# Modulation columns by two transposes per step, with shift and scale formed on VectorE

## The chip, the core and the metric

The kernel runs on one core of a Trainium2 chip. The metric is the device time of one execution in microseconds (us). Three runs of the kernel before took 601.96, 602.42 and 602.82 us, so the median is 602.42 us. The engines are named as the profile names them: PE is TensorE's matmul, PEld its weight load, DVE is VectorE, ACT is ScalarE, POOL is GpSimd, SP is SyncE, whose queue issues most of the transfers here.

## What is computed

One layer of a diffusion trunk: an adaLN-modulated RMSNorm, an input projection, two head groups (a gated position mixer and a latent attention), and an output projection. Only the modulation matters here. For each of the two conditioning vectors, `c` for 1024 latent tokens and `c_ctx` for 128 context tokens:

```python
mod = jax.nn.silu(cond) @ w_ada + b_ada
shift, scale, gate = jnp.split(mod[:, None, :], 3, axis=-1)
h = _rmsnorm(x, norm_g) * (1 + scale) + shift
u, v, g_a, c_q, c_kv, k_rope, g_b = _split_in(h @ w_in)
```

The width is 1024, handled as eight blocks of 128 channels (k = 0 to 7). Each token tile is transposed, so that channels lie on partitions; shift and scale of a block are therefore wanted as columns, one number per partition.

## The kernel before

The change lies in the start of the program, roughly its first 50 us. There are nine token tiles of 128 (g = 0 is tiles 0 to 2, g = 1 tiles 3 to 5, g = 2 tiles 6 to 8). For each block k the start does the following.

- **rows** (`mod_rows`, L337): eight products of the conditioning vector's columns (`csp`, padded with zeros to 32 columns) with the modulation weights (`ada`) go to four strips of 32 partitions in `modp`, columns 0 to 255, each strip holding the sum over two of the eight input blocks. In a strip, row 0 belongs to one conditioning vector, row 1 to the other, and the rest is zero.
- **copy** (`mod_copy`, L341): DVE copies these 256 columns to SBUF (`rows`).
- **cols** (`mod_cols`, L345): two f32 matmuls with `rows` as weights and `sel` (a 128x2 matrix of ones that picks row 0 or 1 of each strip) as the moving operand add the four strips and turn them to columns at once. They write `modp[:, 256:260]`.
- **act** (`mod_act`, L348 and L349): two ACT operations read these columns from PSUM and make shift and scale in `at`, the first by adding a bias, the second by a scale and a bias.
- **hh, hf, lo**: ACT applies `at` to the transposed tile (L571, rounded to fp32r, the high part), ACT or DVE does it again in f32 (L578 on ACT, L580 on DVE), and DVE subtracts to get the low part (L112).
- **va, vb**: PE multiplies the high parts (L431, L432) and the low parts (L436) of the tiles with the weights of v, which accumulate over k in the banks `vacc`. Those weights are split by POOL into a high part (**wh**, L115) and a low part (**wl**, L550).

The transposes of the token tiles (L353) are `xT` and `xe`; they use tiles that were first scaled by the RMSNorm root (**sc**: L389 on ACT, L393 on DVE, L391 on POOL). For tiles 3 to 5 these go to ACT, DVE and POOL in turn (the constant `SC1 = "SVG"`).

All of this shares one PSUM bank, `modp`. From block 2 on, one step of the planner, `group(k)`, issues cols of k, the transposes of group 1, and rows of k+1, in this order, and act of k is issued behind them.

The order on each engine is not written by hand. `start_steps` lists steps with an engine, a cost, dependencies and a priority; `Plan.run` plays them forward against these costs and issues each step when its turn comes. A changed cost or engine in the list thus changes the order of other steps too, and each engine then keeps its order whatever the chip does. The SP queue issues loads in a fixed order, and a load into a buffer that is still read waits at the head of that queue: the weights of v for block k+2 (`wvr`, L309) wait for wl of block k, and the modulation weights behind them wait as well.

Of the kernel before, what the change touches and what calls it, by code (L numbers as in the profile page):

```python
# [9 lines left out]
F32 = mybir.dt.float32  # L10
# [3 lines left out]
AF = mybir.ActivationFunctionType  # L14
ALU = mybir.AluOpType
AX = mybir.AxisListType
PSUM = bass.MemoryType.PSUM

P = 128
NT = 9  # L20
NS = 8
NK = 8
# [72 lines left out]
def tile_hymba_step(ctx: ExitStack, tc: tile.TileContext, I, O):  # L95
    nc = tc.nc
    V, S, G, T = nc.vector, nc.scalar, nc.gpsimd, nc.tensor

    def opened(name, bufs=1, space=None, side=None):
        kw = dict(name=name, bufs=bufs, reuse_waits="tile")  # L100
        if space is not None:
            kw["space"] = space
        if side is not None:
            kw["side"] = side
        cm = tc.tile_pool(**kw)
        return cm, cm.__enter__()
# [4 lines left out]
    def lo_of(lo, src, hi):  # L111
        V.tensor_tensor(lo, src, f32(hi), op=ALU.subtract)  # L112
# [58 lines left out]
    def catch_up(until):  # L171
        at_ = now[0]
        while waiting and waiting[0][0] <= until:
            due, fn = waiting.pop(0)
            now[0] = due
            fn()
        now[0] = at_
# [9 lines left out]
    def step(cost, fn):  # L187

        catch_up(now[0])
        for f in list(fill):  # L190
            if f[0] in made and made_at[f[0]] <= now[0]:
                fill.remove(f)
                run(f[1:])
        run((cost, fn))
# [12 lines left out]
    def run(step):  # L207
        catch_up(now[0])
        step[1]()
        now[0] += step[0]  # L210
# [23 lines left out]
    ident = pc.tile([P, P], F32, tag="ident", name="ident")  # L234
# [8 lines left out]
    normg = cst[:, 16:24]  # L243
    badaT = cst[:, 24:48].rearrange("p (k j) -> p k j", j=3)
# [3 lines left out]
    at = pc.tile([P, 8, 2, 2], F32, tag="at", name="at")  # L248
    gbias = pc.tile([P, 8], F32, tag="gbias", name="gbias")
# [13 lines left out]
    c_vb, vb = opened("vb", side="left")  # L263
# [12 lines left out]
    sel = va.tile([P, 2], F32, tag="sel", name="sel")  # L276
# [51 lines left out]
    mps, rowsb = {}, {}  # L328

    modp = psa.tile([P, 512], F32, tag="acc", name="modp")  # L330

    def mod_rows(k, i):


        for j in range(4):
            kk = 4 * i + j
            T.matmul(modp[32 * j : 32 * j + 32, 0:256], csp[:, kk, :], ada[k][kk], start=i == 0, stop=i == 1)  # L337

    def mod_copy(k):
        rowsb[k] = va.tile([P, GW], F32, tag="tm", name=f"rows{k}", bufs=2)[:, :256]  # L340
        V.tensor_copy(rowsb[k], modp[:, 0:256])  # L341

    def mod_cols(k):
        for c in range(2):
            T.matmul(modp[:, 256 + 2 * c : 258 + 2 * c], rowsb[k][:, c * P : (c + 1) * P], sel, start=True, stop=True)  # L345

    def mod_act(k):
        S.activation(at[:, k, :, 0], modp[:, 256:258], AF.Identity, bias=badaT[:, k, 0:1])  # L348
        S.activation(at[:, k, :, 1], modp[:, 258:260], AF.Identity, bias=gbias[:, k : k + 1], scale=normg[:, k : k + 1])  # L349

    def transposes(k, ts_, ps):
        for j, t in enumerate(ts_):
# [54 lines left out]
    def h_pe(k, g):  # L407
        xps[k, g] = pst.tile([P, 512], F32, tag="t", name=f"xT{k}{g}")
        transposes(k, [3 * g, 3 * g + 1, 3 * g + 2], xps[k, g])
# [24 lines left out]
    def last_product(k, t):  # L434
        g, j = t // 3, t % 3
        T.matmul(vacc[t], hl[k, g][:, j * P : (j + 1) * P], wvh[k], start=False, stop=False)  # L436
# [3 lines left out]
    def keep_warm(n):  # L440
        for _ in range(n):
            T.matmul(warm[:, 0:P], ident, ones, start=True, stop=True)

    def start_steps(plan):
        step = plan.add
# [95 lines left out]
        def split_hi(k):  # L541
            wvh[k] = wide(1024 * k, 512)
            if k == 0:
                S.copy(wvh[k], wvr[k])
            else:
                pool_copy(wvh[k], wvr[k])

        def split_lo(k):
            wvl[k] = wide(1024 * k + 512, 512)
            G.tensor_tensor(wvl[k], wvr[k], f32(wvh[k]), op=ALU.subtract)  # L550
# [3 lines left out]
        def both_rows(k):  # L554
            mod_rows(k, 0)
            mod_rows(k, 1)

        def group(k):
            mod_cols(k)
            h_pe(k, 1)  # L560
            if k + 1 < NK:
                both_rows(k + 1)

        def plan_alias(key, *others):
            for o in others:
                plan.alias.setdefault(key, []).append(o)

        def high(k, g):
            src = first_t(k) if g == 0 and k > 0 else xps[k, g][:, :GW]
            b_, a_ = at[:, k, 0, 0:1], at[:, k, 0, 1:2]  # L570
            S.activation(hh[k, g], src, AF.Identity, bias=b_, scale=a_)  # L571
# [10 lines left out]
        for k in range(NK):  # L582
            q = 0.1 * k
            step(f"wh{k}", "S" if k == 0 else "G", 0.62, lambda k=k: split_hi(k), [f"wv{k}"], 1 + q)
            step(f"wl{k}", "G", 1.28, lambda k=k: split_lo(k), [f"wh{k}"], 1 + q)
            if k == 0:
                step("fill", "T", 0.0, lambda: keep_warm(2), ["rows0.1"], 0)
                for i in range(2):
                    step(f"rows0.{i}", "T", 0.45, lambda i=i: mod_rows(0, i), [f"ada0.{i}", *(["rows0.0"] if i else [])], 1)
                step("cols0", "T", 0.5, lambda: mod_cols(0), ["copy0"], 0)  # L590
            elif k == 1:
                step("rows1.1", "T", 0.7, lambda: both_rows(1), ["ada1.0", "ada1.1", "copy0", "cols0"], 1.1)
            step(f"copy{k}", "V", 0.42, lambda k=k: mod_copy(k), [f"rows{k}.1"], 0.2 + q)
            if k == 1:
                step("cols1", "T", 0.5, lambda: mod_cols(1), ["copy1", "act0"], 1.0)
                for q_ in range(2):
                    step(f"xt{q_}1", "T", 0.36, lambda q_=q_: h_pe(q_, 1), [*scaled[1], "cols1"], 1.1 + 0.1 * q_, takes=("pst",))
                step("rows2.0", "T", 0.45, lambda: mod_rows(2, 0), ["copy1", "ada2.0", "xt11"], 1.2)
                step("rows2.1", "T", 0.45, lambda: mod_rows(2, 1), ["rows2.0", "ada2.1", "va03"], 1.2)
            elif k > 1:  # L600

                step(
                    f"cols{k}", "T", 0.8 + (0.65 if k + 1 < NK else 0.0), lambda k=k: group(k),
                    [f"copy{k}", f"act{k - 1}", *scaled[1], *([f"ada{k + 1}.{i}" for i in range(2)] if k + 1 < NK else [])], 1 + q, takes=("pst",),
                )
                plan_alias(f"cols{k}", f"xt{k}1", *([f"rows{k + 1}.1"] if k + 1 < NK else []))
            step(f"act{k}", "S", 0.6, lambda k=k: mod_act(k), [f"cols{k}"], 0.2 + q)
            for g in range(2):
                pre = g == 0 and k > 0
                if k == 0 and g == 0:  # L610
                    step(f"xt{k}{g}", "T", 0.36, lambda k=k, g=g: h_pe(k, g), [*scaled[g], *([f"act{k - 1}"] if k > 1 else [])], 2 + q, takes=("pst",))
                src = f"xs{k}" if pre else f"xt{k}{g}"
                e_ = FULL[g] if k else "SV"[g]
                step(f"hh{k}{g}", "S", 0.6, lambda k=k, g=g: high(k, g), [src, f"act{k}"], 2 + q)
                last = () if pre else ("pst",)
                step(f"hf{k}{g}", e_, {"S": 0.6, "V": 0.66, "G": 0.6}[e_], lambda k=k, g=g, e_=e_: full(k, g, e_), [src, f"act{k}", f"hh{k}{g}", *([f"lo{k}0"] if g and k > 3 else [])], 2.05 + q, gives=last)
                step(f"lo{k}{g}", "V", 0.58, lambda k=k, g=g: lo_of(hl[k, g], hf[k, g], hh[k, g]), [f"hf{k}{g}"], 2.1 + q)
                if k == NK - 1:
                    continue
                for t in (0, 1, 2) if g == 0 else (3, 4):  # L620
                    before = [f"va{k - 1}{t}"] if k else []
                    if (k, t) == (1, 0):
                        before.append("va03")
                    step(f"va{k}{t}", "T", 0.46, lambda k=k, t=t: first_products(k, t), [f"hh{k}{g}", f"wl{k}", *before], 3 + q + 0.001 * t, takes=("psa",) if k == 0 else ())
                    step(f"vb{k}{t}", "T", 0.23, lambda k=k, t=t: last_product(k, t), [f"lo{k}{g}", f"va{k}{t}"], 3 + q + 0.01 + 0.001 * t)

    engines = {mybir.EngineType.PE, mybir.EngineType.Activation, mybir.EngineType.DVE, mybir.EngineType.Pool}
    with tc.manual_schedule(engines=engines):
        keep_warm(WARM0)
        start = Plan()  # L630
# [9 lines left out]
    step = plan.add  # L640
# [589 lines left out]
    for g in range(3):  # L1230
        q = area[g].rearrange("p (s h) c -> p s h c", s=4)
# [830 lines left out]
    step = plan.add  # L2062
# [111 lines left out]
    for q in range(3, len(queue)):  # L2174
        n, name, _ = queue[q]
# [278 lines left out]
```

## Time and profile before

| | us |
|---|---|
| median of three runs | 602.42 (601.96 to 602.82) |
| the profiled execution's own time | 602.15 |
| its span, first to last instruction | 600.4 |
| PE busy | 590.3 |
| DVE busy | 427.3 |
| ACT busy | 329.2 |
| POOL busy | 214.0 |

The profiled execution lies 1.75 us above its own span and 0.27 us below the median. A row of a timeline reads: start, duration, engine, line, operation, output<-inputs, the number merged, and in brackets how long the engine had been idle and what released it. Consecutive matmuls overlap, so the distance between starts, not the duration, is what one costs.

### The profile page before, as it was taken

The page shows a single profiled execution, that of the slowest core. Times are in us where ns is not written, and L with a number is a line of the kernel's source. Part 1 is how long each engine was busy: PE and PEld are TensorE (multiplying, and loading weights), DVE is VectorE, ACT ScalarE, POOL GpSimd, SP SyncE. Part 2 cuts the span into 40 slices and gives each one's busy share as a digit, 9 for nine tenths or more (in the row PEclk, how much of TensorE's full clock was granted, in tenths as well). Part 3 has the DMA queues.
Part 4 walks back from the last instruction along what each step waited for, and adds up shares of the span by engine and source line. Part 5 has one row for each costly group of instructions (what it writes and reads, how often), then busy time and mean ns, then how long its engine had stood idle before and what let it go on. Part 6 is the DMA issues. An engine that isn't in the chain of part 4 may idle for free.

```text
span 600.4 us, 10191 instructions
## 1 busy us (share of the span) xinstructions
PE 590.3 (98%) x3661; PEld 528.2 (88%) x3661; DVE 427.3 (71%) x940; ACT 329.2 (55%) x773; POOL 214.0 (36%) x251
## 2 busy tenths in 40 slices
PE   9999999999999999999999999999999999999995
PEld 8578889999989999999998888888888898888884
DVE  4666888977647368476678677778788876477885
ACT  6565886434323245465577566656656462457543
POOL 2571103200000000343363345454544547269834
PEclk9999999999999999999999999999999999999998
DMA  8991001032052134100002033434242029951444
GB/s 319 370 370 70 1 2 70 1 140 71 4 212 69 69 93 138 43 1 0 2 8 71 0 106 106 157 126 141 81 143 94 1 72 303 361 178 41 144 147 160
DMA packets 31059, 67.33 MB, mean 112 GB/s; under 512 B 3344, under 2 KB 17440, under 8 KB 29984
## 3 DMA queue, kind: packets, MB, share of 16 engines
q1 hardware_dynamic: 27792, 55.93, 26.9%
q0 software_dynamic: 2352, 8.39, 4.1%
q10 hardware_dynamic: 864, 2.36, 1.1%
q8 instruction: 29, 0.48, 0.3%
q14 instruction: 22, 0.18, 0.1%
HBM read 53.45 MB, written 13.21 MB: 111 GB/s over the span
## 4 chain that ended last, share of the span: by engine, by line
PE 93%; DMA 3%; DVE 2%; ACT 1%; POOL 1%; issue 0%; SPq 0%; POOLq 0%; ACTq 0%
PE p L916 14%; PE tp L937 7%; PE pT L1586 6%; PE o L1610 3%; PE o L1612 3%; PE o L1611 3%; PE zacc L1349 2%; PE zacc L1348 2%; PE zacc L1350 2%; PE S L1947 2%; PE S L1948 2%; PE S L1949 2%; DMA ada<-in_ada_ss 2%; PE s L1503 2%; PE s L1506 2%; PE s L1505 2%
## 5 line engine op out<-in xcount | busy, mean ns | idle before, releaser
L1463 POOL TENSOR_SCALAR e<-e,rs 128x1280 f32<-128x1280 f32 x32 | 47.0, 1468 | 97.2 <-DVE rs L1462 62.8
L112 DVE TENSOR_TENSOR pl<-pT,ph 128x512 fp32r<-128x512 f32 x81 | 55.5, 687 | 32.5 <-ACT ph L1590 32.2
L1458 ACT ACTIVATE e<-s,nb,scl 128x256 f32<-128x256 f32 x64 | 56.9, 890 | 38.9 <-DVE nb L1446 26.2
L1590 ACT CAST ph<-pT 128x512 fp32r<-128x512 f32 x80 | 47.1, 589 | 40.8 <-PE pT L1586 40.6
L1196 POOL TENSOR_TENSOR kr<-z,rope 128x64 f32<-128x64 f32 x8 | 2.6, 324 | 155.3 <-ACT z L1205 155.3
L937 PE MATMUL tp<-area,w 128*128 128x384 f32 x288 | 52.6, 338 | 0.0
L1610 PE MATMUL o<-ph,vh 128*128 128x256 f32 x160 | 50.7, 317 | 0.0
L937 PEld LDWEIGHTS tp<-area,w 128*128 128x128 f32 x288 | 50.4, 188 | 0.0
L1586 PE MATMUL pT<-ident,e 128*128 128x128 f32 x320 | 48.0, 273 | 0.0
L1586 PEld LDWEIGHTS pT<-ident,e 128*128 128x128 f32 x320 | 38.9, 140 | 7.2
L1612 PE MATMUL o<-ph,vl 128*128 128x256 f32 x160 | 45.1, 282 | 0.0
L1611 PE MATMUL o<-pl,vh 128*128 128x256 f32 x160 | 44.9, 280 | 0.0
L1440 DVE TENSOR_REDUCE m<-s 128x1 f32<-128x1024 f32 x32 | 39.0, 1218 | 2.6 <-PE s L1481 2.5
L1610 PEld LDWEIGHTS o<-ph,vh 128*128 128x128 f32 x160 | 30.2, 189 | 4.7 <-ACT os L1620 2.9
L1611 PEld LDWEIGHTS o<-pl,vh 128*128 128x128 f32 x160 | 30.4, 190 | 0.4
L1612 PEld LDWEIGHTS o<-ph,vl 128*128 128x128 f32 x160 | 30.1, 188 | 0.0
L916 PE MATMUL p<-area,w 128*128 128x384 f32 x144 | 27.7, 339 | 0.0
L916 PE MATMUL p<-area,s 128*128 128x384 f32 x144 | 27.3, 337 | 0.0
L1348 PE MATMUL zacc<-w1t,area 128*128 128x448 f32 x72 | 27.1, 376 | 0.0
L916 PE MATMUL p<-w1t,s 128*128 128x384 f32 x144 | 26.9, 339 | 0.0
L1349 PE MATMUL zacc<-w1t,area 128*128 128x448 f32 x72 | 26.3, 366 | 0.0
L1350 PE MATMUL zacc<-w1t,area 128*128 128x448 f32 x72 | 26.3, 365 | 0.0
(697 smaller groups left out, 1770.4 us busy)
## 6 DMA issues: line engine op xcount, KB each, us to landing
ada<-in_ada_ss SPq DMA_DIRECT2D x16, 512.0 KB, 6.0
w2r<-in_w_t SPq DMA_DIRECT2D x12, 512.0 KB, 5.1
x<-in_x SPq DMA_DIRECT2D x9, 512.0 KB, 8.4
adag<-in_ada_g SPq DMA_DIRECT2D x4, 1024.0 KB, 4.8
traw<-in_w_o SPq DMA_DIRECT2D x16, 256.0 KB, 3.8
tdram<-thi SPq DMA_DIRECT2D x32, 128.0 KB, 1.9
tdram<-traw SPq DMA_DIRECT2D x32, 128.0 KB, 1.8
wor<-in_w_o SPq DMA_DIRECT2D x8, 512.0 KB, 3.8
```

Source lines behind the costliest of these rows:

```text
L112: V.tensor_tensor(lo, src, f32(hi), op=ALU.subtract)
L916: T.matmul(banks[key], a_, b_, start=k == 0 and m == 0, stop=k == 3 and m == len(passes) - 1)
L937: T.matmul(tps[c, 2][:, :GW], w_[c][:, k, :], x_[k, 2], start=k == 0 and m == 0, stop=k == NK - 1 and m == 2)
L1348: T.matmul(ps[:, :448], a, wqh[k], start=k == 0, stop=False)
L1440: V.tensor_reduce(m[:, 0:1], lat_, axis=AX.X, op=ALU.max)
L1458: S.activation(e[:, sl], src, AF.Exp, bias=nb, scale=scl[:, t : t + 1], accum_out=su[:, i : i + 1])
L1463: G.tensor_scalar(e, e, rs, 0.0, op0=ALU.mult, op1=ALU.add)
L1586: T.transpose(ps[:, w : w + P], es[t, h][:, c * P : (c + 1) * P], ident)
L1590: later(0.5, lambda: S.copy(ph[:, :w], ps[:, :w]))
L1610: T.matmul(o, vh[:, kt, :], ph[:, sl], start=c == 0, stop=False)
L1611: T.matmul(o, vh[:, kt, :], pl[:, sl], start=False, stop=False)
L1612: T.matmul(o, vl[:, kt, :], ph[:, sl], start=False, stop=c == n - 1)
```

## The change

The diff, whole:

```diff
     def mod_cols(k):
         for c in range(2):
-            T.matmul(modp[:, 256 + 2 * c : 258 + 2 * c], rowsb[k][:, c * P : (c + 1) * P], sel, start=True, stop=True)
+            T.transpose(modp[:, 256 + c * P : 256 + (c + 1) * P], rowsb[k][:, c * P : (c + 1) * P], ident)
 
     def mod_act(k):
-        S.activation(at[:, k, :, 0], modp[:, 256:258], AF.Identity, bias=badaT[:, k, 0:1])
-        S.activation(at[:, k, :, 1], modp[:, 258:260], AF.Identity, bias=gbias[:, k : k + 1], scale=normg[:, k : k + 1])
+        m = vb.tile([P, 2, 2], F32, tag="mods", name=f"mods{k}", bufs=2)
+        V.tensor_reduce(m, modp[:, 256:512].rearrange("p (a j c) -> p a c j", a=2, j=4)[:, :, 0:2, :], axis=AX.X, op=ALU.add)
+        V.tensor_scalar(at[:, k, :, 0], m[:, 0, :], badaT[:, k, 0:1], None, op0=ALU.add)
+        V.tensor_scalar(at[:, k, :, 1], m[:, 1, :], normg[:, k : k + 1], gbias[:, k : k + 1], op0=ALU.mult, op1=ALU.add)
...
-                step("cols0", "T", 0.5, lambda: mod_cols(0), ["copy0"], 0)
+                step("cols0", "T", 0.35, lambda: mod_cols(0), ["copy0"], 0)
...
-                step("cols1", "T", 0.5, lambda: mod_cols(1), ["copy1", "act0"], 1.0)
+                step("cols1", "T", 0.35, lambda: mod_cols(1), ["copy1", "act0"], 1.0)
...
-                    f"cols{k}", "T", 0.8 + (0.65 if k + 1 < NK else 0.0), lambda k=k: group(k),
+                    f"cols{k}", "T", 0.65 + (0.65 if k + 1 < NK else 0.0), lambda k=k: group(k),
...
-            step(f"act{k}", "S", 0.6, lambda k=k: mod_act(k), [f"cols{k}"], 0.2 + q)
+            step(f"act{k}", "V", 0.55, lambda k=k: mod_act(k), [f"cols{k}"], 0.2 + q)
```

The two matmuls with `sel` become two transposes of the same rows, which fill columns 256 to 511 of `modp` with four strips side by side. DVE adds the strips (a reduction of 16 numbers to 4 on each partition) and forms shift and scale with two small operations; ACT's two are gone. The planner is told that cols costs 0.15 less and that act is on DVE at 0.55. Lines behind L346 move down by two in the changed kernel (L550 becomes L552, L391 L393, L353 L355, L431 to L436 become L433 to L438; L580 becomes L582).

The planner's order moves at three places that matter here.

POOL, early in the start: `x2` and `x5` are token tiles being scaled (sc), `wvr0` to `wvr2` the weights of v for blocks 0 to 2. Before:

```order
L391 TENSOR_SCALAR x2_165<-x2_165,x3r_182 128x1024 [waits DMAHW3_49,DVE_49,Activation_49]
L550 TENSOR_TENSOR w1t_121<-wvr0_189,w1t_121 128x512 [waits DMAHW6_49,Activation_49]
L391 TENSOR_SCALAR x5_228<-x5_228,x3r_276 128x1024 [waits DMAHW1_49,DVE_49,Activation_49]
L115 TENSOR_SCALAR w1t_121<-wvr1_283 128x512 [waits DMAHW4_49]
L550 TENSOR_TENSOR w1t_121<-wvr1_283,w1t_121 128x512 [waits Pool_49]
```

POOL at the same place of the changed kernel:

```order
L393 TENSOR_SCALAR x2_165<-x2_165,x3r_182 128x1024 [waits DMAHW3_49,DVE_49,Activation_49]
L552 TENSOR_TENSOR w1t_121<-wvr0_189,w1t_121 128x512 [waits DMAHW6_49,Activation_49]
L115 TENSOR_SCALAR w1t_121<-wvr1_280 128x512 [waits DMAHW4_49]
L393 TENSOR_SCALAR x5_234<-x5_234,x3r_273 128x1024 [waits DMAHW1_49,DVE_49,Activation_49]
L552 TENSOR_TENSOR w1t_121<-wvr1_280,w1t_121 128x512 [waits Pool_49]
```

The scaling of tile 5 has moved behind the split wh of block 1, which waits for a transfer.

PE from cols of block 1 on (`xT01` is the transposed group 1 for block 0; its third tile waits for POOL). Before:

```order
L345 MATMUL modp_122<-sel_116,rows1_302 128x2 [waits DVE_49]
L345 MATMUL modp_122<-sel_116,rows1_302 128x2
L353 MATMUL xT01_313<-ident_75,x3_198 128x128 [waits Activation_49]
L353 MATMUL xT01_313<-ident_75,x4_207 128x128 [waits DVE_49]
L353 MATMUL xT01_313<-ident_75,x5_228 128x128 [waits Pool_49]
L353 MATMUL xT11_317<-ident_75,x3_198 128x128
L353 MATMUL xT11_317<-ident_75,x4_207 128x128
L353 MATMUL xT11_317<-ident_75,x5_228 128x128
L337 MATMUL modp_122<-ada20_293,csp_110 32x256 [waits DMAHW5_49,Activation_49]
L337 MATMUL modp_122<-ada20_293,csp_110 32x256 x3
L431 MATMUL vacc3_331<-w1t_121,area1_119 128x512 [waits Activation_49]
L432 MATMUL vacc3_331<-w1t_121,area1_119 128x512
```

PE at the same place of the changed kernel:

```order
L345 MATMUL modp_122<-ident_75,rows1_304 128x128 [waits DVE_49]
L345 MATMUL modp_122<-ident_75,rows1_304 128x128
L355 MATMUL xT01_318<-ident_75,x3_198 128x128 [waits Activation_49]
L355 MATMUL xT01_318<-ident_75,x4_207 128x128 [waits DVE_49]
L355 MATMUL xT01_318<-ident_75,x5_234 128x128 [waits Pool_49]
L355 MATMUL xT11_325<-ident_75,x3_198 128x128
L355 MATMUL xT11_325<-ident_75,x4_207 128x128
L355 MATMUL xT11_325<-ident_75,x5_234 128x128
L337 MATMUL modp_122<-ada20_295,csp_110 32x256 [waits DMAHW5_49,DVE_49]
L337 MATMUL modp_122<-ada20_295,csp_110 32x256 x3
L433 MATMUL vacc1_247<-w1t_121,area0_118 128x512 [waits Activation_49]
L434 MATMUL vacc1_247<-w1t_121,area0_118 128x512 [waits Pool_49]
```

The first product behind the transposes is now one of block 1 (`vacc1`), which waits for POOL's wl of block 1; before, it was one of block 0 on group 1 (`vacc3`), which needs ACT alone. The transposes, up to the third tile of `xT01` and its wait for POOL, stand where they did.

DVE around blocks 2 and 3 of the changed kernel (`mods` holds the four sums; `area` is a low part, `mixA` an f32 tile):

```order
L349 TENSOR_REDUCE mods2_389<-modp_122 128x4 [waits PE_49]
L350 TENSOR_SCALAR at_86<-mods2_389,cst_84 128x2 [waits DVE_49]
L351 TENSOR_SCALAR at_86<-mods2_389,cst_84,gbias_87 128x2
L341 COPY rows3_395<-modp_122 128x256
L582 TENSOR_SCALAR mixA_95<-xT21_370,at_86 128x384 [waits DVE_49,Activation_49]
L112 TENSOR_TENSOR area0_118<-mixA_95,area0_118 128x384 [waits Activation_49]
L349 TENSOR_REDUCE mods3_429<-modp_122 128x4 [waits PE_49]
```

Before, the copy of block 3 stood at this place with waits of its own, and shift and scale were made by two operations on ACT:

```order
L341 COPY rows3_389<-modp_122 128x256 [waits PE_49,Activation_49]
L580 TENSOR_SCALAR mixA_95<-xT21_367,at_86 128x384 [waits Activation_49]
L112 TENSOR_TENSOR area0_118<-mixA_95,area0_118 128x384 [waits Activation_49]
L341 COPY rows4_427<-modp_122 128x256 [waits DVE_49,PE_49,Activation_49]
```

The copy has lost its wait for ACT, and the reduction ahead of it now carries the wait for PE, which covers the copy's as well: it is the wait for the rows of the next block. The order on the SP queue is the same in both kernels.

## The prediction

> **What bounds the kernel now.** I read first the busy shares of the page, then the chain of work that ended last, then the stretches of the start one by one.
>
> ```profile
> PE 590.3 (98%) x3661; PEld 528.2 (88%) x3661; DVE 427.3 (71%) x940; ACT 329.2 (55%) x773; POOL 214.0 (36%) x251
> PE 93%; DMA 3%; DVE 2%; ACT 1%; POOL 1%; issue 0%; SPq 0%; POOLq 0%; ACTq 0%
> ```
>
> PE is busy 98% of the span and holds 93% of the chain. A busy PE need not be PE at its peak, so the next view asks what PE waits for where the change lies, from 19 to 62 us. Columns: engine and line waiting, what released it, total us, times, longest.
>
> ```profile
> PE modp L337 <- DMA ada<-in_ada_ss: 0.6, 1, 0.6
> PEld modp L337 <- DMA ada<-in_ada_ss: 1.1, 1, 1.1
> PEld vacc L431 <- ACT area L571: 0.4, 1, 0.4
> PEld modp L345 <- DVE rows L341: 0.3, 1, 0.3
> PEld xT L353 <- DVE x L393: 0.2, 1, 0.2
> ACT at L348 <- PE modp L337: 9.0, 5, 4.0
> DVE rows L341 <- ACT at L349: 4.7, 4, 2.2
> ```
>
> The waits on DMA are for the modulation weights of block 1. After them every wait of PE for another engine is one short stall, and together they are under 1 us. ACT waits 9.0 us for PE before it forms shift and scale, and DVE waits 4.7 us for ACT before its copy. So from about 22 us PE runs through in its own order, and what counts is (1) how much PE work a step has and (2) whether the new order makes PE wait. Time freed on ACT is worth nothing by itself.
>
> **The PE work removed.** The rows of block 4's cols (starts and durations in us), and the same place seen over the whole kernel:
>
> ```profile
> 33.29 0.50 PE L345 MATMUL modp<-sel,rows 128*128 128x2 f32 x4
> 33.65 0.52 PE L353 MATMUL xT<-ident,x 128*128 128x128 f32 x3
> L345 PE MATMUL modp<-sel,rows x32: 165/251/272, 12.0 to 44.1; 128*128 128x2 f32 x32
> L353 PE MATMUL xT<-ident,x x27: 272/273/331, 12.4 to 44.5; 128*128 128x128 f32 x27
> 12.81 1.47 PE L353 MATMUL xe<-ident,x 128*128 128x128 f32 x12
> 19.69 0.55 PE L353 MATMUL xe<-ident,x 128*128 128x128 f32 x3
> ```
>
> Sixteen calls of L345 gave 32 instructions: an f32 matmul is two passes, however narrow its output. The 27 transposes of `xT` are 27 instructions, one pass each. Cols is therefore four passes, from 33.29 to 33.65 or 0.36 us; afterwards it is two. What two cost is the spacing of transposes: three starts span 0.52 less one duration of 0.273, over two gaps, 0.125 each. The twelve of `xe` give (1.47 - 0.273) / 11 = 0.109, the three at 19.69 give 0.14. So two cost 0.25 (bounds 0.22 and 0.28) and a step saves 0.11 to 0.12 (bounds 0.08 and 0.14). I take 0.115.
>
> Of eight steps, block 0 saves nothing, since PE then still has the wait for block 1's modulation weights before it (0.6 and 1.1 us above); nor does block 1, since the transposes behind its cols wait for tile 4, which DVE scales until 20.99 (rows below). That leaves six, blocks 2 to 7: 6 x 0.115 = **0.69 us saved** (0.5 to 0.84).
>
> **Shift and scale on DVE instead of ACT.** Step 4 as it is, and DVE's small operations:
>
> ```profile
> 31.10 0.97 PE L436 MATMUL vacc<-w1t,area 128*128 128x512 f32 x3
> 31.24 0.26 ACT L348 ACTIVATE at<-modp,cst 128x2 f32<-128x2 f32 x1 [0.91 <-PE modp L337]
> 31.40 0.34 ACT L349 ACTIVATE at<-modp,gbias,cst 128x2 f32<-128x2 f32 x1
> 31.78 0.43 DVE L341 COPY rows<-modp 128x256 f32<-128x256 f32 x1 [0.86 <-ACT at L349]
> 62.04 0.17 DVE L122 TENSOR_SCALAR vv3t<-vv3v 128x12 int32<-128x12 int32 x1
> 62.25 0.17 DVE L123 TENSOR_SCALAR vv3r<-vv3t 128x12 int32<-128x12 int32 x1
> 62.33 0.17 DVE L124 TENSOR_SCALAR vv3w<-vv3v 128x12 f32<-128x12 f32 x1
> ```
>
> ACT's two operations start when the rows of the next block end, although cols was done more than a microsecond earlier, and the high part starts 0.54 later (31.78). The order shows that the reduction on DVE carries the same wait, so a faster cols doesn't bring it forward. A dependent small operation follows after 0.21 (62.04 to 62.25), an independent one after 0.08, and lasts 0.17: reduction, first and second operation take 0.21 + 0.08 + 0.17 = 0.46, which matches ACT's 0.54. A small reduction out of PSUM isn't in this trace. It costs DVE between 0.16 (the small operations above) and 0.43 (the copy of 256 columns at 31.78, sixteen times its data); I take 0.17. Even the upper end makes the high parts only 0.2 later, and PE, busy with products queued ahead, waited for ACT just once, 0.4 us. The copy, which no longer waits for ACT, starts at 31.24 + 0.21 + 0.08 + 0.08 = 31.61, 0.17 earlier. Price at PE: **0**, with that one stall deeper by 0.2 or shallower by 0.1 as the bounds. If the cover of queued products went, it would be up to 0.2 in each of six steps. ACT loses eight times 0.54 us of work, beside 9.0 us of waiting there: 0.
>
> **What the new order costs.** POOL now splits the weights of block 1 before it scales tile 5:
>
> ```profile
> 9.87 0.75 DVE L393 TENSOR_SCALAR x<-x,x3r 128x1024 f32<-128x1024 f32 x1
> 10.01 1.60 POOL L391 TENSOR_SCALAR x<-x,x3r 128x1024 f32<-128x1024 f32 x1 [8.70 <-DVE x3r L404]
> 18.07 1.12 POOL L391 TENSOR_SCALAR x<-x,x3r 128x1024 f32<-128x1024 f32 x1 [4.66 <-DVE x3r L404]
> 19.83 0.62 POOL L115 TENSOR_SCALAR w1t<-wvr 128x512 fp32r<-128x512 f32 x1 [0.64 <-DMA wvr<-in_w_v]
> 20.53 1.58 POOL L550 TENSOR_TENSOR w1t<-wvr,w1t 128x512 fp32r<-128x512 f32 x1
> 20.16 0.83 DVE L393 TENSOR_SCALAR x<-x,x3r 128x1024 f32<-128x1024 f32 x1
> 21.05 0.53 PEld L353 LDWEIGHTS xT<-ident,x 128*128 128x128 f32 x5 [0.16 <-DVE x L393]
> 21.74 0.16 PEld L337 LDWEIGHTS modp<-ada,csp 128*32 128x32 f32 x8 [0.17 <-issue]
> 22.65 0.40 PE L432 MATMUL vacc<-w1t,area 128*128 128x512 f32 x1
> 26.95 1.28 POOL L550 TENSOR_TENSOR w1t<-wvr,w1t 128x512 fp32r<-128x512 f32 x1
> 30.42 1.65 POOL L550 TENSOR_TENSOR w1t<-wvr,w1t 128x512 fp32r<-128x512 f32 x1
> ```
>
> Before, tile 5 was scaled at 18.07, in time (19.19). Now it stands behind a split that can't start until its weights land at 19.83, so it starts at 20.53, where wl of block 1 started. It lasted 1.12 alone and 1.60 when DVE's L393 overlapped its first 0.61 us; here L393 covers 0.46 (20.53 to 20.99), so 1.12 + 0.48 x 0.46 / 0.61 = 1.48, and it ends at 22.01. The third transpose of `xT01` then loads at about 22.06. From there to the weight load of L337 there are four loads at (0.53 - 0.14) / 4 = 0.10 apart and the 0.17 shown: three gaps, 0.14 and 0.17 make 0.60, so 22.66 in place of 21.74. PE loses **0.92 us**, with bounds 0.56 (1.12) and 1.04 (1.60).
>
> The rule of the Trainium skill for this overlap ("SBUF — State Buffer", section "Who interferes with whom") is that whoever of VectorE in a two-port mode and GpSimd issues first keeps the shared port pair for its whole instruction and the other is fully blocked. By it the scaling at 10.01 would have lasted 0.61 + 1.12 = 1.73, while the row has 1.60; here it would end at 20.99 + 1.12 = 22.11, the loss would be 1.02 and the sum 0.1 higher.
>
> Behind it, wl of block 1 runs from 22.1, for 1.28 to 1.65, to 23.4 to 23.75. The new first product waits for it in its second pass, which stood at 22.65 and would come at 23.57: a wait of 0 to 0.2. DVE has no subtraction ready there, so I take 1.28 and 0.
>
> **Sum:** 0.92 - 0.69 + 0 = +0.23 us, from 0.56 - 0.84 - 0.1 = -0.4 to 1.04 + 0.2 - 0.5 + 0.2 = +0.9. From about 62 us on both kernels have the same instructions in the same order, chained to PE, so I carry this to the end: a profiled 602.15 would become 602.38, and the median 602.42 becomes **602.65**. With the 0.4 that the runs spread, the forecast alone spans 601.6 to 603.7.
>
> **Rivals.**
> - *The order costs nothing.* If wvr lands earlier than in the profiled run, or tile 5 is otherwise in time, only the saving remains: 602.42 - 0.69 = 601.7. For it: the wait of POOL there is only 0.64 us long. Against: tile 5 would have to start 1.4 us earlier, and the transfers of that time are queued without a gap.
> - *The transposes save nothing*, as when their own weight loads hold them to what the four passes took: 602.42 + 0.92 = 603.3. Against: the spacings above.
> - *DVE falls behind: slower.* Place: DVE between the rows of one block and the cols of the next. Each step adds 0.46 us there.
>
> ```profile
> 33.67 2.11 DVE L112 TENSOR_TENSOR area<-mixA,area 128x384 fp32r<-128x384 f32 x2
> 35.11 0.50 PE L431 MATMUL vacc<-w1t,area 128*128 128x512 f32 x1
> 35.78 0.43 DVE L341 COPY rows<-modp 128x256 f32<-128x256 f32 x1
> 36.82 0.50 PE L345 MATMUL modp<-sel,rows 128*128 128x2 f32 x4
> ```
>
>  Once, already, two subtractions held DVE until 35.78, 0.67 past the end of the rows (35.11). The copy must end before PE has done its products between rows and cols; seven took from 35.11 to 36.82, 1.7 us, and the new order has at least seven. Reduction, the two small operations and copy need 0.37 + 0.43 or, with the gap to the rows' end, 0.9, so it decides from 0.8 us of lateness on. If 0.67 grows by the added 0.46, it is past that at once, and PE then pays those 0.46 in each of the four steps left: 602.65 + 1.8 = 604.4. Against: the 4.7 us that DVE waited in these steps.
> - *The transfers thin out.* wl of block 1 ends 1.3 to 1.65 later, the load of block 3's weights waits for it on SP's queue, and the modulation weights of block 4 stand behind that load.
>
> ```profile
> 22.56 0.86 SPq L463 DMA_DIRECT2D ada<-in_ada_ss  x2
> DMA to landing us min/median/max: 6.0/6.0/6.9
> 30.10 1.07 PE L337 MATMUL modp<-ada,csp 128*32 128x256 f32 x16
> ```
>
>  The second of the two, issued at 22.99, landed at 29.0 to 29.9 and would land at 30.3 to 31.5, if all of the delay comes through. PE wants it at 30.10 + 0.92, less what blocks 2 and 3 saved (0.23), so 30.8: up to 0.7 more, 603.3. Against: transfers already queued ahead of it hide part of the delay.
>
> **Chances.** The forecast 0.60, the order for nothing 0.13, the transposes for nothing 0.07, DVE behind 0.13, the transfers 0.07. A measurement of this kernel tells about 0.2%, 1.2 us, from no change: faster is below 601.2, slower above 603.6. Only DVE falling behind ends well above, with the top of the two at 603.3 slower 0.15; only the low end of the first rival lies below, faster 0.07; the rest, 0.78, is the same. The range drops the DVE case and the lowest tail: 601.7 less 0.4 is 601.3, and 603.3 with 0.4 to 0.5 is 603.8.
>
> **What would show it.** Cols as two PE instructions a step, 0.25 us from its first start to that of `xT`; L393 on POOL starting near 20.5 with PE's loads of `xT` stalled on it until about 22.0; the copy with no wait for ACT; the reduction starting when the rows end; no stall of PE on DVE or ACT from 24 to 60 us. The forecast is wrong if POOL scales tile 5 by 19.5, if cols on PE keeps 0.36, or if PE's loads of L345 wait for DVE in several steps.

## The result, and the profile after

The changed kernel is slower: 604.27 us median (603.98 to 605.06, 8 runs) against 602.33 us (601.94 to 602.82, 8 runs), a ratio of 1.0031 with a 95% interval of 1.0023 to 1.0040. That is 1.9 us more, where 0.23 more was forecast; 604.27 lies above the forecast range of 601.3 to 603.8.

The page of the changed kernel, busy shares and the chain that ended last:

```profile
PE 590.4 (98%) x3645; PEld 526.6 (87%) x3645; DVE 436.7 (72%) x964; ACT 325.2 (54%) x757; POOL 212.0 (35%) x251
PE 88%; DVE 4%; DMA 3%; ACT 2%; POOL 2%; issue 0%; SPq 0%; POOLq 0%; DVEq 0%; ACTq 0%
```

PE has lost 16 instructions (the second pass of sixteen matmuls) and works as long as before, but its part of the chain fell from 93% to 88%: DVE, ACT and POOL have come onto it. Four rows of the waits from 19 to 64 us say where (waiting engine and line, releaser, total us, times, longest):

```profile
PE modp L345 <- DVE rows L341: 1.0, 1, 1.0
PE vacc L433 <- ACT area L573: 0.8, 1, 0.8
PE xT L355 <- POOL x L393: 0.6, 1, 0.6
ACT area L573 <- DVE at L351: 16.3, 7, 4.1
```

The third was forecast. The first two are new: PE waits for a copy of DVE, and for ACT, which itself waits for shift and scale. The timeline at the first place, block 1:

```profile
20.01 0.62 POOL L115 TENSOR_SCALAR w1t<-wvr 128x512 fp32r<-128x512 f32 x1 [6.57 <-DMA wvr<-in_w_v]
20.61 1.55 POOL L393 TENSOR_SCALAR x<-x,x3r 128x1024 f32<-128x1024 f32 x1
21.10 0.15 DVE L349 TENSOR_REDUCE mods<-modp 128x4 f32<-128x16 f32 x1
21.29 0.89 DVE L350 TENSOR_SCALAR at<-mods,cst 128x2 f32<-128x2 f32 x1
22.08 1.33 DVE L351 TENSOR_SCALAR at<-mods,cst,gbias 128x2 f32<-128x2 f32 x1
22.13 1.26 POOL L552 TENSOR_TENSOR w1t<-wvr,w1t 128x512 fp32r<-128x512 f32 x1
22.80 0.16 PEld L337 LDWEIGHTS modp<-ada,csp 128*32 128x32 f32 x8 [0.17 <-issue]
23.45 0.71 ACT L573 ACTIVATE area<-mixA,at 128x384 fp32r<-128x384 f32 x1 [2.51 <-DVE at L351]
24.21 0.50 PE L433 MATMUL vacc<-w1t,area 128*128 128x512 f32 x1 [0.78 <-ACT area L573]
```

Two operations on two numbers per partition, which last 0.23 and 0.28 us in most steps, take 0.89 and 1.33 here. Each ends just behind an operation of POOL: L350 at 22.18, POOL's scaling at 22.16; L351 at 23.41, POOL's subtraction at 23.39. POOL was also at work at block 0 (subtraction until 13.45), and there the first operation ends at 13.47:

```profile
12.89 0.58 DVE L350 TENSOR_SCALAR at<-mods,cst 128x2 f32<-128x2 f32 x1
```

PE loses 0.2 us there, but waits 0.49 for a transfer afterwards (rows at 19.31), so it hardly matters. The second place where it does is shift and scale of block 6, with the copy for block 7 behind them:

```profile
44.08 2.37 POOL L115 TENSOR_SCALAR w<-w2r 128x1024 fp32r<-128x1024 f32 x2
45.23 0.23 DVE L350 TENSOR_SCALAR at<-mods,cst 128x2 f32<-128x2 f32 x1
45.37 1.11 DVE L351 TENSOR_SCALAR at<-mods,cst,gbias 128x2 f32<-128x2 f32 x1
46.38 0.41 DVE L341 COPY rows<-modp 128x256 f32<-128x256 f32 x1
46.84 0.44 PE L345 MATMUL modp<-ident,rows 128*128 128x128 f32 x2 [0.96 <-DVE rows L341]
```

POOL's second operation ends at 46.45, L351 at 46.48; the copy behind it is late, and PE's cols of block 7 waits 0.96. Block 3, with POOL idle, shows the two operations undisturbed:

```profile
33.14 0.16 DVE L349 TENSOR_REDUCE mods<-modp 128x4 f32<-128x16 f32 x1
33.34 0.23 DVE L350 TENSOR_SCALAR at<-mods,cst 128x2 f32<-128x2 f32 x1
33.48 0.28 DVE L351 TENSOR_SCALAR at<-mods,cst,gbias 128x2 f32<-128x2 f32 x1
```

And cols, from its start to that of the next rows, is now 0.64 (27.50 to 28.14), where it was 0.81 (33.29 to 34.10):

```profile
27.50 0.38 PE L345 MATMUL modp<-ident,rows 128*128 128x128 f32 x2
27.71 0.49 PE L355 MATMUL xT<-ident,x 128*128 128x128 f32 x3
28.14 1.07 PE L337 MATMUL modp<-ada,csp 128*32 128x256 f32 x16
```

Of the kernel before, the sum below needs these rows (first product behind block 1's transposes, rows behind cols of block 4, first transpose of the last token group); the fourth is that transpose in the changed kernel:

```profile
22.32 0.50 PE L431 MATMUL vacc<-w1t,area 128*128 128x512 f32 x1
34.10 1.07 PE L337 MATMUL modp<-ada,csp 128*32 128x256 f32 x16
59.61 0.49 PE L353 MATMUL h<-ident,x 128*128 128x128 f32 x3
61.76 0.49 PE L355 MATMUL h<-ident,x 128*128 128x128 f32 x3
```

So the two traces give: first product behind block 1's transposes 22.32 to 24.21, or 1.89 later, of which 0.19 is the transfer ahead (rows at 19.31 instead of 19.12), 0.87 POOL's new order (rows of block 2 at 22.80 instead of 21.74, less 0.19) and 0.83 the wait for shift and scale; six cols at 0.17 less, -1.0; and 0.96 at block 7. Together +1.85. Where the start ends, at the first transpose of the last token group, the shift is 2.15 (59.61 to 61.76), 0.3 more. The first run below, with PE's order unchanged, shows that the two waits for DVE cost that much more than the idle times counted here.

### The profile page after: what moved, and what is told of

It is laid out like the page before. It is cut to its first block, busy times and chain, and to the rows that moved or that the text cites. A ratio compares the mean times of both kernels' runs of the same rounds, so it can differ in the third digit from the quotient of the medians.

```text
span 602.7 us, 10159 instructions
## 1 busy us (share of the span) xinstructions
PE 590.4 (98%) x3645; PEld 526.6 (87%) x3645; DVE 436.7 (72%) x964; ACT 325.2 (54%) x757; POOL 212.0 (35%) x251
## 4 chain that ended last, share of the span: by engine, by line
PE 88%; DVE 4%; DMA 3%; ACT 2%; POOL 2%; issue 0%; SPq 0%; POOLq 0%; DVEq 0%; ACTq 0%
PE p L918 15%; PE tp L939 7%; PE pT L1588 5%; PE o L1612 3%; PE o L1614 3%; PE o L1613 3%; PE zacc L1351 2%; PE zacc L1352 2%; PE zacc L1350 2%; PE S L1951 2%; PE S L1950 2%; PE S L1949 2%; DMA ada<-in_ada_ss 2%; PE s L1505 2%; PE s L1508 2%; PE s L1507 2%
```

## The experiments

Two theories went into the runs. Theory 1: an operation of POOL on SBUF holds up those of VectorE that read and write SBUF. Theory 2: the long operations are waits that the new order of the program brings. Each kernel was timed beside the kernel before, in two sessions; the median of the kernel before was 602.17 us (33 runs) for the first four and 602.41 (29 runs) for the last three. Each ratio is to the kernel before of the same session.

### Sums in PSUM

```diff
-        m = vb.tile([P, 2, 2], F32, tag="mods", name=f"mods{k}", bufs=2)
+        m = modp[:, 264:268].rearrange("p (c a) -> p c a", c=2)
```

> The four sums go to unused columns of the same PSUM bank instead of SBUF; the order on every engine is that of the changed kernel. Theory 1 (while POOL runs an operation on SBUF, a VectorE operation whose tensor operands both lie in SBUF is held up to its end): with the source in PSUM both small operations last under 0.35 us in all eight steps, PE's waits at 24.2 us (0.8) and 46.8 us (1.0) go, its wait on POOL near 22.2 us stays; 604.3 - 1.8 = 602.5 us. Theory 2 (the lengths of 0.9, 1.3 and 1.1 us are waits for data or for readers of the columns that the new order brings): they stay, 604.3 us.

Measured: 601.89 us median (601.38 to 603.5, 11 runs), ratio 0.9996 (0.9988 to 1.0005). The two operations in all eight steps (ns: shortest, median, longest):

```profile
L350 DVE TENSOR_SCALAR at<-modp,cst x8: 203/219/221, 12.8 to 47.4; 128x2 f32<-128x2 f32 x8
L351 DVE TENSOR_SCALAR at<-modp,cst,gbias x8: 263/270/272, 12.9 to 47.6; 128x2 f32<-128x2 f32 x8
PE xT L355 <- POOL x L393: 0.6, 1, 0.6
```

In the changed kernel the longest were 893 and 1335. With the same order on every engine, the same reduction and the same arithmetic, only the place of four numbers moved, and 2.4 us went (604.27 to 601.89; 2.2 when each is set against the kernel before of its own session). The wait of PE for POOL stays, as theory 1 has it. Theory 2 falls. The gain is more than the 1.8 that I had worked out from the two waits. PE runs the same 172 matmuls from the rows of block 2 to cols of block 7 in both kernels:

```profile
22.23 0.64 PE L337 MATMUL modp<-ada,csp 128*32 128x256 f32 x8
44.16 0.38 PE L345 MATMUL modp<-ident,rows 128*128 128x128 f32 x2
```

That is 21.93 us here and 24.04 in the changed kernel (22.80 to 46.84), so the two waits cost 2.1. The idle time of a row is counted from the recorded end of the matmul ahead of it, and where PE doesn't wait the next one starts before that end (here the row ahead of cols of block 7 ends at 44.33, and cols starts at 44.16); so 0.78 and 0.96 understate the price.

### Tile 5 first

```diff
-            step(f"wh{k}", "S" if k == 0 else "G", 0.62, lambda k=k: split_hi(k), [f"wv{k}"], 1 + q)
+            step(f"wh{k}", "S" if k == 0 else "G", 0.62, lambda k=k: split_hi(k), [f"wv{k}", *(["sc5"] if k == 1 else [])], 1 + q)
```

> The split of block 1's weights is made to wait for the scaling of tile 5, which puts POOL back into the order of the kernel before; the sums stay in SBUF. Theory 1: PE's wait on POOL near 22 us goes and the first product needs no new columns, so about 1.9 us come back there, but the first small operation of block 1 is still held by POOL's subtraction (to about 22.2 us) and PE's wait of 1.0 us at 46.8 us stays; 602.4 us. Theory 2: the small operations are short again with the old order, both waits go, 604.3 - 2.9 = 601.4 us.

Measured: 602.47 us (601.8 to 603.05, 11 runs), ratio 1.0003 (0.9994 to 1.0012). It is theory 1's figure, though PE's wait of 1.0 us has become two. POOL's subtraction now meets the first operation of block 1:

```profile
20.76 1.58 POOL L552 TENSOR_TENSOR w1t<-wvr,w1t 128x512 fp32r<-128x512 f32 x1
21.34 1.03 DVE L350 TENSOR_SCALAR at<-mods,cst 128x2 f32<-128x2 f32 x1
22.29 0.28 DVE L351 TENSOR_SCALAR at<-mods,cst,gbias 128x2 f32<-128x2 f32 x1
27.74 0.74 DVE L350 TENSOR_SCALAR at<-mods,cst 128x2 f32<-128x2 f32 x1
39.29 0.80 DVE L350 TENSOR_SCALAR at<-mods,cst 128x2 f32<-128x2 f32 x1
44.49 1.11 DVE L351 TENSOR_SCALAR at<-mods,cst,gbias 128x2 f32<-128x2 f32 x1
PE modp L345 <- DVE rows L341: 0.7, 2, 0.4
```

L350 ends at 22.37, POOL's operation at 22.34. Five of the sixteen operations are held here: these four and L350 of block 0 (0.77). In the changed kernel it was four, in blocks 0, 1 (both) and 6; blocks 2 and 5 are new, and the second operation of block 1 is free. In each kernel it is those that meet an operation of POOL before its last 0.2 us. At block 1 being held now costs PE nothing, since products are queued there; but PE waits for a late copy twice, at cols of blocks 4 and 7, 0.7 us together.

### Both

The two edits above together.

> Sums in PSUM and POOL in the order of before. Theory 1: no long small operation, no wait of PE on POOL, and cols in 0.64 instead of 0.81 us up to the next rows leaves six steps' saving, 602.3 - 1.0 = 601.3 us. Theory 2: the source of the operands is without effect, so the same time as with tile 5 first and the sums in SBUF.

Measured: 601.32 us (600.78 to 601.99, 11 runs), ratio 0.9984 (0.9975 to 0.9993): faster than both kernels, 0.85 us below the kernel before. Tile 5 is scaled in time, and of the waits of PE's matmuls in this stretch only those for a transfer and for tile 4 are left:

```profile
18.05 1.12 POOL L393 TENSOR_SCALAR x<-x,x3r 128x1024 f32<-128x1024 f32 x1 [4.66 <-DVE x3r L406]
PE modp L337 <- DMA ada<-in_ada_ss: 0.7, 1, 0.7
PE xT L355 <- DVE x L395: 0.2, 1, 0.2
```

PE's matmuls no longer wait for a copy. The difference to the previous kernel, 1.15 us, is the source of the operands alone. The difference to sums in PSUM, 0.57, is what POOL's old order, with the few products on PE that move along with it, gives back.

### Cols by the matrix of ones, shift and scale on VectorE

```diff
-            T.transpose(modp[:, 256 + c * P : 256 + (c + 1) * P], rowsb[k][:, c * P : (c + 1) * P], ident)
+            T.matmul(modp[:, 256 + 2 * c : 258 + 2 * c], rowsb[k][:, c * P : (c + 1) * P], sel, start=True, stop=True)
...
+        V.tensor_scalar(at[:, k, :, 0], modp[:, 256:258], badaT[:, k, 0:1], None, op0=ALU.add)
+        V.tensor_scalar(at[:, k, :, 1], modp[:, 258:260], normg[:, k : k + 1], gbias[:, k : k + 1], op0=ALU.mult, op1=ALU.add)
```

The reduction and its tile are gone.

> Cols as before (four passes with the matrix of ones, which add the strips), and VectorE forms shift and scale straight from PSUM, without a reduction; the planner's costs are those of the changed kernel, so is the order. Theory 1: no long small operation; as with sums in PSUM, but six steps cost 0.17 more each on PE: 602.5 + 1.0 = 603.5 us. Theory 2: the long operations stay, 604.3 + 1.0 = 605.3 us.

Measured: 603.11 us (602.56 to 604.29, 11 runs), ratio 1.0017 (1.0008 to 1.0026). Theory 1 again (603.5 expected, 605.3 by theory 2): the longest second operation is 274 ns, as this row shows.

```profile
L349 DVE TENSOR_SCALAR at<-modp,cst,gbias x8: 264/271/274, 13.3 to 45.7; 128x2 f32<-128x2 f32 x8
```

Against sums in PSUM, which has the same order on PE and POOL, this kernel is 1.22 us slower: that is what the transposes save on PE, 0.2 in each of six steps. The 0.17 a step from the traces gives 1.0; the two agree within the intervals of the ratios.

### Shift and scale on ScalarE, from sums in SBUF

```diff
-        V.tensor_scalar(at[:, k, :, 0], m[:, 0, :], badaT[:, k, 0:1], None, op0=ALU.add)
-        V.tensor_scalar(at[:, k, :, 1], m[:, 1, :], normg[:, k : k + 1], gbias[:, k : k + 1], op0=ALU.mult, op1=ALU.add)
+        S.activation(at[:, k, :, 0], m[:, 0, :], AF.Identity, bias=badaT[:, k, 0:1])
+        S.activation(at[:, k, :, 1], m[:, 1, :], AF.Identity, bias=gbias[:, k : k + 1], scale=normg[:, k : k + 1])
```

> Transposes and the reduction on VectorE into SBUF stay; ScalarE forms shift and scale from the sums in SBUF. Order on PE and POOL as in the changed kernel. Theory 1 (POOL holds up VectorE operations with both tensor operands in SBUF): ScalarE is not held, its two operations last 0.25 to 0.35 us in all eight steps, and the reduction, which reads PSUM, 0.16; like the kernel with sums in PSUM, with a hop between engines of about 0.3 more in front of the high parts, which PE's queued products cover: 602.0 us, at most 602.5. Rival (anything that reads the sums right behind the reduction while POOL works is late, on whichever engine): long operations or waits of 1 us stay, 604.3 us.

Measured: 602.64 us (601.97 to 603.37, 11 runs), ratio 1.0002 (0.9994 to 1.0011). A little above the 602.5 that I had as the most, but far from 604.3, and nothing is held:

```profile
L349 DVE TENSOR_REDUCE mods<-modp x8: 155/174/175, 13.1 to 47.2; 128x4 f32<-128x16 f32 x8
L350 ACT ACTIVATE at<-mods,cst x8: 295/295/298, 13.3 to 47.4; 128x2 f32<-128x2 f32 x8
L351 ACT ACTIVATE at<-mods,gbias,cst x8: 372/372/374, 13.5 to 47.6; 128x2 f32<-128x2 f32 x8
```

The same numbers in SBUF, read while POOL does the same work, don't delay ScalarE. They were not late either: it is VectorE that is held. PE's stretch from the rows of block 2 to cols of block 7 takes 21.93 us (22.67 to 44.60), as with the sums in PSUM. So the 0.5 us by which this kernel is slower than that one (0.23 above and 0.28 below the kernel before of its session) lies outside this stretch; where stays open.

### One element at a time

```diff
-        V.tensor_scalar(at[:, k, :, 0], m[:, 0, :], badaT[:, k, 0:1], None, op0=ALU.add)
-        V.tensor_scalar(at[:, k, :, 1], m[:, 1, :], normg[:, k : k + 1], gbias[:, k : k + 1], op0=ALU.mult, op1=ALU.add)
+        for c in range(2):
+            V.tensor_scalar(at[:, k, c : c + 1, 0], m[:, 0, c : c + 1], badaT[:, k, 0:1], None, op0=ALU.add)
+            V.tensor_scalar(at[:, k, c : c + 1, 1], m[:, 1, c : c + 1], normg[:, k : k + 1], gbias[:, k : k + 1], op0=ALU.mult, op1=ALU.add)
```

> The sums stay in SBUF, and VectorE makes shift and scale by four operations of one element per partition in place of two of two. Theory 1a (an operation is held by POOL because it splits its two elements over both ports): with one element nothing is held, every operation lasts under 0.3 us, 602.2 us. Theory 1b (any VectorE operation on SBUF of this kind is held, whatever its size): one or two of the four last 0.9 to 1.3 us at block 1 and one at block 7, 604.3 us or a little more.

Measured: 602.31 us (601.97 to 602.7, 11 runs), ratio 0.9999 (0.9990 to 1.0007). Theory 1a. All four operations run beside the operation of POOL that held L350 in the changed kernel:

```profile
20.63 1.55 POOL L394 TENSOR_SCALAR x<-x,x3r 128x1024 f32<-128x1024 f32 x1
21.31 0.21 DVE L351 TENSOR_SCALAR at<-mods,cst 128x1 f32<-128x1 f32 x1
21.44 0.27 DVE L352 TENSOR_SCALAR at<-mods,cst,gbias 128x1 f32<-128x1 f32 x1
21.62 0.20 DVE L351 TENSOR_SCALAR at<-mods,cst 128x1 f32<-128x1 f32 x1
21.74 0.26 DVE L352 TENSOR_SCALAR at<-mods,cst,gbias 128x1 f32<-128x1 f32 x1
```

Twice as many operations, out of SBUF, are 2.0 us faster than two. PE's stretch takes 21.93 again (22.82 to 44.75). So an SBUF source alone doesn't make VectorE wait; it takes more than one element. Theory 1a's reason, that two elements are shared out over both ports, isn't shown by these runs: they show that one element is free and two are held.

### The kernel before, with POOL's new order

```diff
-                step(f"sc{t}", sc_[j], {"S": 1.15, "V": 0.78, "G": 1.5}[sc_[j]], lambda t=t, j=j, e_=sc_[j], cell=cell: scale_x(E[e_], t, cell["r"][:, j : j + 1]), [f"r{n}"], p_)
+                step(f"sc{t}", sc_[j], {"S": 1.15, "V": 0.78, "G": 1.5}[sc_[j]], lambda t=t, j=j, e_=sc_[j], cell=cell: scale_x(E[e_], t, cell["r"][:, j : j + 1]), [f"r{n}", *(["wh1"] if t == 5 else [])], p_)
```

> The kernel before, with the one edit that the scaling of tile 5 waits for the split of block 1's weights, so that POOL has the order of the changed kernel. If the order costs what the prediction said, PE waits for POOL at the third transpose of block 0's second group and the time is 602.2 + 0.9 = 603.1 us (with block 1's subtraction late, up to 603.3); if it costs nothing, 602.2 us.

Measured: 603.23 us (603.12 to 605.9, 12 runs), ratio 1.0016 (1.0007 to 1.0024), 0.82 us above its kernel before. PE waits where it was expected:

```profile
PE xT L353 <- POOL x L391: 0.6, 1, 0.6
```

The profiled execution of this kernel was its slowest (605.9), with the transfer ahead about a microsecond late; only the place of the wait is read from it, not the price.

## Why the prediction was wrong

**The step that failed** is "Shift and scale on DVE instead of ACT", priced at 0 with bounds of -0.1 and 0.2. It took 0.17 us for each small operation, from rows at 62 us where POOL is idle, and asked only whether VectorE and ScalarE had time, relying on products queued on PE to cover the rest. It didn't ask what POOL does then, although the next part weighed just this overlap for the scaling of tile 5 and used two rows that showed it (1.60 and 1.12 us for the same work). What the runs showed in its place: POOL holds these operations by up to 1.05 us (1.33 instead of 0.28). At two of the steps where the changed kernel meets this, PE has too little queued: behind block 1's transposes, where the new order had put a product that needs these columns first, and at cols of block 7. Taking the sums to PSUM removes 2.4 us (2.2 against each session's kernel before) with the order unchanged; with POOL's old order it removes 1.15. Undisturbed, the reduction and the two operations take 0.62 (33.14 to 33.76) where 0.46 was forecast, but that costs nothing: with the sums in PSUM they take as long, and PE's matmuls don't wait for them. The other steps:

- **The PE work removed**, 0.69 us (0.5 to 0.84), was too small. The mechanism was right (four passes become two); by the two traces a step saves 0.17, by the timing of sums in PSUM against the matrix of ones 1.22 us in six steps, with a DVE reduction more on the faster side. The spacing of other transposes had given 0.25 from cols to the first transpose of `xT`; it is 0.21 (27.50 to 27.71). The following rows come 0.02 sooner still, which the step didn't count.
- **The new order on POOL**, 0.92 us (0.56 to 1.04), holds: 0.82 us when done alone to the kernel before, and 0.87 between the two traces. With the sums in PSUM it is worth 0.57. The scaling lasted 1.55, against 1.48 forecast. The rival "The order costs nothing" asked for tile 5 to start 1.4 us earlier; by the prediction's own sum about 0.9 would do. POOL started it at 20.61.
- **The wait for block 1's subtraction**, 0 to 0.2, wasn't reached: PE was already waiting for ACT.
- **The sum without the failed step.** The kernel with sums in PSUM is the changed kernel without it: 601.89, or 0.28 below its kernel before, where +0.23 was forecast, inside the -0.4 to +0.9 given for it. The transposes saved more and the order cost less than forecast.
- **The rival "DVE falls behind"** came near in time (604.4) and in place (PE's cols waiting for the copy, 0.96 us at block 7), but not in its cause: nothing grew by 0.46 a step. Lateness came in single blows from POOL, one of them at a product and not at a copy.
- **The rule of the Trainium skill** that the prediction cites ("SBUF — State Buffer", section "Who interferes with whom") covers the new operations too: whoever issues first keeps the shared port pair for its whole instruction, and a `tensor_scalar` can enter a two-port mode. The rows agree where VectorE is held: it goes on when POOL's operation ends, each time. Which of the two issued first isn't readable in one of them, since the row of L351 of block 1 starts 0.04 before POOL's subtraction (22.08 and 22.13), behind an L350 still running until 22.18. For POOL's own scaling behind VectorE's of tile 4 (20.36 to 21.17) the rule would give 0.56 + 1.12 = 1.68, where the row has 1.55. That a source in PSUM, or a single element, isn't held is shown by the runs. The rule was applied to POOL's large operation, which VectorE could delay, and not to VectorE's small ones, which POOL could.

## What to carry to other kernels

When work is moved to VectorE, price it against what GpSimd does at that moment: an operation of 0.2 us on SBUF can be held for the rest of a GpSimd operation (about 1 us here), and everything queued behind it on VectorE pays as well. Where it sits on a path, try its source in PSUM or one element at a time, both of which were free here, and compare the order that the planner makes on every engine, since the second loss here lay on one that the edit doesn't mention. A short operation's duration should be read from rows in which the neighbouring engine is busy too.

## What the hardware showed beyond that

- Being small doesn't protect an operation: two numbers per partition waited up to 1.05 us, as the rest of POOL's operation left it. The held operations end 0.02 to 0.03 us after the recorded end of POOL's (22.18 and 22.16, 23.41 and 23.39, 46.48 and 46.45) though they need 0.23 to 0.28 undisturbed. If they take that once released, they begin 0.2 to 0.25 us before that end, and POOL's recorded spans run somewhat past the release. L350 of block 6 fits: it starts 0.21 before the end of a POOL operation (45.44) and lasts its usual 0.23.
- A reduction of 16 numbers out of PSUM was never held: 154 to 175 ns in all eight steps of the changed kernel.
- ScalarE takes 295 and 372 ns to form shift and scale from SBUF, and 262 and 347 from PSUM.
